# Down stage: parts of three pairs of steps held behind the last unit, the residual queued behind the loads, three pieces of sums moved there

## The chip, the core and the metric

One core of a Trainium2 chip runs the program. The core has a matrix engine (PE, with PEld for its weight loads), three engines for elementwise work (DVE, ACT, POOL), a queue engine for transfers (SP) and 16 transfer engines. Each engine takes its own instructions in the order in which they were built; an instruction that waits holds up all that stand behind it on the same engine. The metric is the device time of one execution in microseconds (us), the median over runs.

## The reference, cut to what matters

One decoder layer over 1024 tokens of width 1024, in float32: three kinds of attention, an output projection, a gated MLP with a short convolution, a gated embedding, a last norm. The change lies in the MLP:

```python
gate = h @ w_gate                       # 1024 x 2816
gate = causal_conv3(gate) + conv_b      # per column, over the last 3 tokens
r = r + (gelu(gate) * (h @ w_up)) @ w_down
```

## The kernel before

Every float32 product is done as three products of a split: an operand x is cast by ACT into a high part (`S.copy`, line 770) and DVE subtracts it from x to get a low part (line 771); `mm3` (lines 115 to 117) then multiplies high by high, high by low, low by high. So every operand that PE reads costs one ACT cast and one DVE subtraction first.

**The gate and up stage.** The 2816 hidden columns are 22 units of 128 (class `Unit` from line 910, its method `rest` from line 932). A unit takes seven products of 12 matmuls (`prod`, line 917): a two-by-two scheme with seven instead of eight block products, in which sums of blocks stand in for the eighth. The products of a unit gather in three banks of PSUM: `a`, `b` and `d`. Bank `b` takes several products one after another and is read in between: after product 7, DVE adds it to `us` (`plus(u1, "b")`, line 945), and product 4 may write into bank `b` only when that is done. Product 3 closes bank `d`, DVE adds it to `gs`, then `conv` (lines 947 to 953) runs on `gs`: ACT scales, DVE adds twice (lines 949, 951), ACT takes the gelu (line 953). DVE multiplies twice (lines 989, 990), and for an odd unit four more subtractions make the sums of the pair. POOL stores the results to DRAM: `hed` for even units, `hod`, `tad`, `tbd` for odd ones.

**The sums of the down weights.** The down projection uses the same scheme, so it needs four sums of blocks of `w_dn`. `sums_down(n, after)` (lines 1006 to 1018) makes one piece of 22: POOL loads a tile `sd` (512 KB), DVE does four operations of 128x256 on it, in the order behind `after`, and POOL stores it to `s_dram`. All pieces share one buffer, so a load waits until the store before it has landed. Unit f makes piece f-1 between its products 7 and 3, from unit 1 on; the last piece, 21, is made when the first 11 steps of the down stage are done.

**The down stage.** 77 steps (line 1062 on): 7 products of 11 steps each, a step being 12 matmuls of 128x512. Two steps make a pair g. `parts(g)` (line 1081) loads the weights of pair g (`wdr`) and, for every second pair, the stored activations of four steps (`hr`), and splits both: `hwd` and `hhd` are the casts on ACT, `lwd` and `lhd` the subtractions on DVE. These carry a raised priority, so the program that sets the order within each engine puts the parts of the first pairs ahead of the end of unit 21. `residual(i)` (line 1104) loads two tiles of the residual r (`rr`) on SP. All loads of the stage go through SP, in order.

`tc.issue_after(x)` puts what is written in its block behind instruction x, if it is on the same engine as x. It adds no semaphore.

Of the kernel before, what the change touches and what calls it, by code (L numbers as in the profile page):

```python
# [73 lines left out]
def trunk(ctx: ExitStack, tc: tile.TileContext, a, out, dbg):  # L74
# [693 lines left out]

    def hl(hi, lo, src, e=V):
        S.copy(hi, src)  # L770
        e.tensor_tensor(out=lo, in0=src, in1=hi.bitcast(F32), op=ALU.subtract)  # L771

    def sum_squares(acc, src, first, cols=slice(0, T), tag="us", e=G):
        if first:
# [16 lines left out]

    he_dram = dp.tile([NJ, P, H2], F32, name="hed")
    ho_dram, ta_dram, tb_dram = [dp.tile([NJ, P, T], F32, name=n) for n in ("hod", "tad", "tbd")]
    s_dram = dp.tile([4, NJ, P, H2], F32, name="sd")
    B = {n: [None] * 4 for n in range(1, 8)}
    acc2 = f4("ws", "acc2")
    r = [f4("r", f"r{d}") for d in range(KD)]
# [112 lines left out]
    class Unit:  # L910
# [21 lines left out]
        def rest(self):  # L932
            f, bank = self.f, self.bank
            gs, cv, us = [f4(t, f"{t}{f}") for t in ("gs", "cv", "us")]
            g0, g1 = [gs[:, half(i)] for i in range(2)]
            u0, u1 = [us[:, half(i)] for i in range(2)]

            def w(j):
                return col(C_CW + 3 * f + j)

            def copy(out, to):
                S.copy(out, bank[to])

            def plus(out, to):
                return V.tensor_tensor(out=out, in0=bank[to], in1=out, op=ALU.add)  # L945

            def conv():
                S.activation(cv, gs, AF.Identity, bias=col(C_CB + f), scale=w(2))
                V.scalar_tensor_tensor(out=cv[:, 1:], in0=gs[:, :T - 1], scalar=w(1), in1=cv[:, 1:],
                                       op0=ALU.mult, op1=ALU.add)  # L950
                V.scalar_tensor_tensor(out=cv[:, 2:], in0=gs[:, :T - 2], scalar=w(0), in1=cv[:, 2:],
                                       op0=ALU.mult, op1=ALU.add)
                S.activation(cv, cv, AF.Gelu_apprx_tanh)

            if f < 3:
                copy(g0, "b")
                plus(g0, "a")
            if f == 0:
                self.prod(5)
                copy(u1, "d")  # L960
                self.prod(3)
                copy(g1, "d")
                self.prod(6)
                plus(g1, "b")
                conv()
                self.prod(7)
                plus(u1, "b")
            else:
                if f > 2:
                    s1 = fp.tile([P, H2], F32, tag="s1", bufs=1, name=f"s1{f}")  # L970
                    self.prod(1)
                    copy(s1, "b")
                    self.prod(5)
                    copy(u1, "d")
                self.prod(6)
                copy(g1, "b")
                if f > 2:
                    self.prod(2)
                    V.tensor_tensor(out=g0, in0=bank["a"], in1=s1, op=ALU.add)
                else:  # L980
                    self.prod(5)
                    copy(u1, "d")
                self.prod(7)
                sums_down(f - 1, plus(u1, "b"))
                self.prod(3)
                plus(g1, "d")
                conv()
            self.prod(4)
            V.tensor_tensor(out=u0, in0=bank["b"], in1=cv[:, half(0)], op=ALU.mult)
            V.tensor_tensor(out=u1, in0=u1, in1=cv[:, half(1)], op=ALU.mult)  # L990
            j = f // 2
            if f % 2 == 0:
                sent[f] = G.dma_start(he_dram[j], u1)
                even.append(us)
                return
            e0, e1 = [even[j][:, half(i)] for i in range(2)]
            t1, t2 = [cv[:, half(i)] for i in range(2)]
            minus(t1, e0, e1)
            minus(t2, u0, t1)
            G.dma_start(ta_dram[j], cv)  # L1000
            minus(e0, u0, e0)
            minus(e1, u1, t2)
            sent[f] = G.dma_start(ho_dram[j], us)
            G.dma_start(tb_dram[j], even[j])

    def sums_down(n, after):

        j, c = n // 2, slice(n % 2 * 256, n % 2 * 256 + 256)
        t = cp.tile([P, 4, 256], F32, tag="rs", bufs=1, name=f"sd{n}")
        with tc.issue_after(sent[n].ins):  # L1010
            G.dma_start(t, a["w_dn"][:, j, :, c].rearrange("b p c -> p b c"))
        a11, a12, a21, a22 = [t[:, i, :] for i in range(4)]
        with tc.issue_after(after.ins):
            V.tensor_tensor(out=a22, in0=a21, in1=a22, op=ALU.add)
            minus(a21, a11, a21)
            minus(a11, a22, a11)
            minus(a12, a12, a11)
        G.dma_start(s_dram[:, j, :, c].rearrange("b p c -> p b c"), t)

    even, sent = [], {}  # L1020
    lft = [t[:, half(0)] for t in r]
# [33 lines left out]
    for f in range(3, NF):  # L1055
        with tc.high_priority(offset=3000):
            raw, A = weights_up_1(f)
            weights_up_2(f, raw, A)
        Unit(f, A).rest()


    steps = [(i, j) for i in DOWN for j in range(NJ)]
# [1 line left out]

    wd = a["w_dn"]
    OPERANDS = {1: (wd[0], he_dram), 2: (wd[1], ho_dram[:, :, half(1)]), 4: (wd[3], tb_dram[:, :, half(1)]),
                6: (s_dram[0], ta_dram[:, :, half(1)]), 3: (s_dram[1], ho_dram[:, :, half(0)]),
                7: (s_dram[2], tb_dram[:, :, half(0)]), 5: (s_dram[3], ta_dram[:, :, half(0)])}

    def load_steps(t, x0, n, which):  # L1070

        x = x0
        while x < x0 + n:
            i, j = steps[x]
            m = min(x0 + n - x, NJ - j)
            nc.sync.dma_start(t[:, x - x0:x - x0 + m, :], OPERANDS[i][which][j:j + m].rearrange("j p t -> p j t"))
            x += m

    LAST = 6 * NJ // 2

    def parts(g):

        with tc.high_priority(offset=300):
# [5 lines left out]
            load_steps(rw, 2 * g, n, 0)  # L1089
            tags = ("whi", "wlo") if g < 2 or g >= LAST and (g - LAST) % 3 else ("r", "r") if g < LAST else ("big", "big")  # L1090
            got = []
            for raw, ts in ((rw, tags), (raws[g // 2][:, g % 2 * 2:g % 2 * 2 + 2, :], ("big", "big"))):
                hi, lo = [f4(t, f"{c}{'wh'[len(got)]}d{g}", (P, 2, H2), F32R) for c, t in zip("hl", ts)]
                hl(hi[:, :n], lo[:, :n], raw[:, :n])
                got.append((hi, lo))
        return got

    r = [None] * KD
# [5 lines left out]
    def residual(i):  # L1104

        t = f4("hx", f"rr{i}", (P, 2, T))
        for d in (2 * i, 2 * i + 1):
            r[d] = t[:, d % 2, :]
            nc.sync.dma_start(r[d], r_dram[d])
        r2.append(t)  # L1110

    def done(d, h):
# [38 lines left out]
    for n, (i, j) in enumerate(steps):  # L1151
        if n % 2 == 0:
            got[n // 2] = parts(n // 2)
        if n in (4, 7, 2 * NJ, 2 * NJ + 4):
            residual((4, 7, 2 * NJ, 2 * NJ + 4).index(n))
        if n > 5 * NJ and todo or todo and j % 2:
            done(*todo.pop(0))
        (wh, wl), (xh, xl) = got[n // 2]
# [7 lines left out]
        if j == NJ - 1:  # L1166
            d0, h = TO[i]
            for d in range(4):
                x = V.tensor_tensor(out=r[d0 + d][:, half(h)], in0=bank[to][d], in1=r[d0 + d][:, half(h)], op=ALU.add)
            if i == 1:  # L1170
                sums_down(NF - 1, x)
            if i in DONE:
                todo += [(DONE[i][0] + d, DONE[i][1]) for d in range(4)]
            if i in (6, 5, 7):
# [178 lines left out]
```

## Time and profile before

| what | value |
|---|---|
| median of 3 runs | 1265.83 us (1265.01 to 1266.31) |
| the profiled execution | 1263.9 us, its span 1262.1 us |
| PE busy | 1233.6 us, 98% of the span |
| DVE busy | 906.5 us, 72% |
| ACT busy | 552.1 us, 44% |
| mean granted PE clock | 0.993 |

The span is what the profiler sees from the first instruction to the last; the execution's own time is 1.8 us longer. Times of single instructions are from the span's start. A busy PE is not a PE at its peak: overlapping matmuls count once, and a matmul at half clock counts in full. So the spacing of the starts of matmuls is read beside the busy time.

### The profile page before, as it was taken

The page shows a single profiled execution, that of the slowest core. Times are in us where ns is not written, and L with a number is a line of the kernel's source. Part 1 is how long each engine was busy: PE and PEld are TensorE (multiplying, and loading weights), DVE is VectorE, ACT ScalarE, POOL GpSimd, SP SyncE. Part 2 cuts the span into 40 slices and gives each one's busy share as a digit, 9 for nine tenths or more (in the row PEclk, how much of TensorE's full clock was granted, in tenths as well). Part 3 has the DMA queues.
Part 4 walks back from the last instruction along what each step waited for, and adds up shares of the span by engine and source line. Part 5 has one row for each costly group of instructions (what it writes and reads, how often), then busy time and mean ns, then how long its engine had stood idle before and what let it go on. Part 6 is the DMA issues. An engine that isn't in the chain of part 4 may idle for free.

```text
span 1262.1 us, 16241 instructions
## 1 busy us (share of the span) xinstructions
PE 1233.6 (98%) x6198; PEld 1034.8 (82%) x6198; DVE 906.5 (72%) x1563; ACT 552.1 (44%) x856; POOL 130.3 (10%) x162
## 2 busy tenths in 40 slices
PE   9999999999999999999999999999989999999996
PEld 7888888888888888878788888888868888888896
DVE  7996967566777477978888878778677545665676
ACT  7324233257675345644433433443353433544432
POOL 2000000011210332001111111111100000000010
PEclk9999999999999999999999999999989999999998
DMA  7100110110102844334555454455689655442132
GB/s 254 51 23 29 35 34 18 34 47 22 34 18 93 322 129 174 100 109 158 188 179 166 158 176 126 155 179 167 209 292 352 213 184 200 141 131 96 42 109 84
DMA packets 61021, 165.02 MB, mean 131 GB/s; under 512 B 6096, under 2 KB 8656, under 8 KB 60944
## 3 DMA queue, kind: packets, MB, share of 16 engines
q1 hardware_dynamic: 43744, 106.44, 25.2%
q0 software_dynamic: 15616, 55.84, 13.2%
q10 hardware_dynamic: 1584, 1.71, 0.4%
q8 instruction: 48, 0.79, 0.3%
q14 instruction: 29, 0.24, 0.1%
HBM read 119.67 MB, written 44.30 MB: 130 GB/s over the span
## 4 chain that ended last, share of the span: by engine, by line
PE 69%; DVE 7%; DMA 3%; ACT 2%; issue 2%; POOL 1%; DVEq 0%; ACTq 0%; POOLq 0%
PE d L116 6%; PE d L115 6%; PE d L117 6%; PE gb L115 5%; PE gb L116 5%; PE gb L117 5%; PE pg L115 2%; PE pg L117 2%; PE pg L116 2%; PE o L115 2%; PE o L117 2%; PE o L116 2%; PE gd L117 2%; PE gd L116 2%; PE gd L115 2%
## 5 line engine op out<-in xcount | busy, mean ns | idle before, releaser
L117 PE MATMUL d<-hhd,lwd 128*128 128x512 f32 x308 | 119.9, 389 | 0.0
L116 PE MATMUL d<-lhd,hwd 128*128 128x512 f32 x308 | 119.9, 389 | 0.0
L115 PE MATMUL d<-hhd,hwd 128*128 128x512 f32 x308 | 119.9, 389 | 0.0
L771 DVE TENSOR_TENSOR lwd<-wdr,hwd 128x1024 fp32r<-128x1024 f32 (+1 forms) x39 | 47.1, 1209 | 56.3 <-ACT hwd L770 55.2
L770 ACT CAST hwd<-wdr 128x1024 fp32r<-128x1024 f32 (+1 forms) x39 | 40.6, 1041 | 94.9 <-PE d L116 78.4
L115 PE MATMUL gb<-b,hf 128*128 128x512 f32 x176 | 70.3, 400 | 6.0 <-DVE us L945 5.6
L115 PE MATMUL gd<-b,f 128*128 128x512 f32 x176 | 68.8, 391 | 1.1 <-ACT f L770 0.6
L116 PE MATMUL gb<-b,hf 128*128 128x512 f32 x176 | 69.5, 395 | 0.0
L117 PE MATMUL gb<-b,lf 128*128 128x512 f32 x176 | 69.4, 394 | 0.0
L117 PE MATMUL gd<-b,f 128*128 128x512 f32 x176 | 68.5, 390 | 0.7 <-DVE f L771 0.7
L116 PE MATMUL gd<-b,f 128*128 128x512 f32 x176 | 68.5, 389 | 0.0
L115 PEld LDWEIGHTS d<-hhd,hwd 128*128 128x128 f32 x308 | 57.9, 188 | 12.2
L117 PEld LDWEIGHTS d<-hhd,lwd 128*128 128x128 f32 x308 | 57.8, 188 | 12.1
L116 PEld LDWEIGHTS d<-lhd,hwd 128*128 128x128 f32 x308 | 57.8, 188 | 11.8
L115 PE MATMUL pg<-hp,hpg 128*128 128x256 f32 (+1 forms) x192 | 61.7, 321 | 0.0
L116 PE MATMUL pg<-lp,hpg 128*128 128x256 f32 (+1 forms) x192 | 61.3, 320 | 0.0
L117 PE MATMUL pg<-hp,lpg 128*128 128x256 f32 (+1 forms) x192 | 61.2, 319 | 0.0
L771 DVE TENSOR_TENSOR lhd<-hr,hhd 128x1024 fp32r<-128x1024 f32 (+1 forms) x39 | 46.7, 1205 | 11.7 <-ACT hhd L770 11.5
L770 ACT CAST f<-wg 128x512 fp32r<-128x512 f32 x22 | 13.8, 625 | 77.6 <-PE gd L117 77.5
L771 DVE TENSOR_TENSOR f<-s,f 128x1024 fp32r<-128x1024 f32 x22 | 26.9, 1224 | 28.5 <-ACT f L770 28.5
L770 ACT CAST hhd<-hr 128x1024 fp32r<-128x1024 f32 (+1 forms) x39 | 39.9, 1037 | 15.0 <-PE d L116 8.5
L115 PEld LDWEIGHTS gb<-b,hf 128*128 128x128 f32 x176 | 33.6, 191 | 15.6 <-DVE us L945 6.5
(459 smaller groups left out, 3498.4 us busy)
## 6 DMA issues: line engine op xcount, KB each, us to landing
wg<-w_gu SPq DMA_DIRECT2D x22, 512.0 KB, 4.4
wu<-w_gu SPq DMA_DIRECT2D x22, 512.0 KB, 3.5
sd<-w_dn POOLq DMA_DIRECT2D x22, 512.0 KB, 5.1
sd<-sd POOLq DMA_DIRECT2D x22, 512.0 KB, 3.9
wdr<-sd SPq DMA_DIRECT2D x20, 512.0 KB, 4.0
wr_wo<-w_out SPq DMA_DIRECT2D x16, 512.0 KB, 3.8
wdr<-w_dn SPq DMA_DIRECT2D x15, 512.0 KB, 4.9
hod<-us POOLq DMA_DIRECT2D x11, 512.0 KB, 2.9
```

Of the source, the lines that this page charges most:

```text
L115: TE.matmul(o, wh, xh, start=first, stop=False, skip_group_check=on)
L116: TE.matmul(o, wh, xl, start=False, stop=False, skip_group_check=on)
L117: TE.matmul(o, wl, xh, start=False, stop=last, skip_group_check=on)
L770: S.copy(hi, src)
L771: e.tensor_tensor(out=lo, in0=src, in1=hi.bitcast(F32), op=ALU.subtract)
```

## The change

`sums_down` in the units is shifted by two: unit f makes piece f-3 from unit 3 on, and units 1 and 2 make none. Pieces 19, 20 and 21 are made in `parts(5)`, `parts(9)` and `parts(13)`, behind the last subtraction of that pair. The load of piece n is queued behind the stores of unit n+2, so that in a given unit it stands where it stood. `s_dram` becomes 11 tensors, one for each pair of pieces, and each load of two steps from it becomes two loads of 256 KB. The casts and subtractions of pairs 2, 3 and 4 are put behind the gelu of unit 21 on ACT and behind its second multiplication on DVE. The loads of the residual are queued on SP behind the loads issued so far, and two of its four calls come two and three steps later.

```diff
     def hl(hi, lo, src, e=V):
         S.copy(hi, src)
-        e.tensor_tensor(out=lo, in0=src, in1=hi.bitcast(F32), op=ALU.subtract)
+        return e.tensor_tensor(out=lo, in0=src, in1=hi.bitcast(F32), op=ALU.subtract)
...
-    s_dram = dp.tile([4, NJ, P, H2], F32, name="sd")
+    s_dram = [dp.tile([4, P, H2], F32, name=f"sd{j}") for j in range(NJ)]
...
-                S.activation(cv, cv, AF.Gelu_apprx_tanh)
+                self.ends = [S.activation(cv, cv, AF.Gelu_apprx_tanh)]
...
-                sums_down(f - 1, plus(u1, "b"))
+                x = plus(u1, "b")
+                if f > 2:
+                    sums_down(f - 3, x)
...
-            V.tensor_tensor(out=u1, in0=u1, in1=cv[:, half(1)], op=ALU.mult)
+            self.ends.append(V.tensor_tensor(out=u1, in0=u1, in1=cv[:, half(1)], op=ALU.mult))
...
-        with tc.issue_after(sent[n].ins):
+        with tc.issue_after(sent[min(n + 2, NF - 1)].ins):
             G.dma_start(t, a["w_dn"][:, j, :, c].rearrange("b p c -> p b c"))
...
-            nc.sync.dma_start(t[:, x - x0:x - x0 + m, :], OPERANDS[i][which][j:j + m].rearrange("j p t -> p j t"))
+            src = OPERANDS[i][which]
+            if isinstance(src, int):
+                m, src = 1, s_dram[j][src]
+            else:
+                src = src[j:j + m].rearrange("j p t -> p j t")
+            sp.append(nc.sync.dma_start(t[:, x - x0:x - x0 + m, :], src if len(src.shape) == 3 else src[:, None, :]))
...
+            if g in (2, 3, 4):
+                held = [tc.issue_after(x.ins) for x in last.ends]
+            else:
+                held = []
+            for x in held:
+                x.__enter__()
             for raw, ts in ((rw, tags), (raws[g // 2][:, g % 2 * 2:g % 2 * 2 + 2, :], ("big", "big"))):
                 hi, lo = [f4(t, f"{c}{'wh'[len(got)]}d{g}", (P, 2, H2), F32R) for c, t in zip("hl", ts)]
-                hl(hi[:, :n], lo[:, :n], raw[:, :n])
+                done_lo = hl(hi[:, :n], lo[:, :n], raw[:, :n])
                 got.append((hi, lo))
+            for x in held[::-1]:
+                x.__exit__(None, None, None)
+            if g in (5, 9, 13):
+                sums_down(NF - 3 + (g - 5) // 4, done_lo)
...
-        for d in (2 * i, 2 * i + 1):
-            r[d] = t[:, d % 2, :]
-            nc.sync.dma_start(r[d], r_dram[d])
+        with tc.issue_after(sp[-1].ins):
+            for d in (2 * i, 2 * i + 1):
+                r[d] = t[:, d % 2, :]
+                nc.sync.dma_start(r[d], r_dram[d])
...
-        if n in (4, 7, 2 * NJ, 2 * NJ + 4):
-            residual((4, 7, 2 * NJ, 2 * NJ + 4).index(n))
+        if n in (6, 10, 2 * NJ, 2 * NJ + 4):
+            residual((6, 10, 2 * NJ, 2 * NJ + 4).index(n))
...
-            if i == 1:
-                sums_down(NF - 1, x)
```

The first place is DVE at the end of unit 21. `us21<-gb21,us21` is the addition that product 4 waits for, `gs21`, `cv21` and the two last `us21` are the rest of the unit, `lhd` and `lwd` are subtractions for the down stage with the number of their pair. Before the change DVE had this row:

```order
L771 TENSOR_TENSOR lwd1_7501<-wdr1_7498,hwd1_7500 128x1024
L771 TENSOR_TENSOR lhd2_7541<-hr2_7532,hhd2_7540 128x1024
L771 TENSOR_TENSOR lhd3_7578<-hr2_7532,hhd3_7577 128x1024
L945 TENSOR_TENSOR us21_7343<-gb21_7345,us21_7343 128x512
L1014 TENSOR_TENSOR sd20_7413<-sd20_7413 128x256
L945 TENSOR_TENSOR gs21_7341<-gd21_7359,gs21_7341 128x512
L876 TENSOR_TENSOR sd20_7413<-sd20_7413 128x256 x3
L771 TENSOR_TENSOR lwd3_7574<-wdr3_7571,hwd3_7573 128x1024
L949 SCALAR_TENSOR_TENSOR cv21_7342<-gs21_7341,small_68,cv21_7342 128x1023
L771 TENSOR_TENSOR lwd4_7614<-wdr4_7611,hwd4_7613 128x1024
L771 TENSOR_TENSOR lwd5_7649<-wdr5_7645,hwd5_7648 128x1024
```

With the change DVE has this row at the same place:

```order
L771 TENSOR_TENSOR lwd1_7497<-wdr1_7494,hwd1_7496 128x1024
L945 TENSOR_TENSOR us21_7339<-gb21_7341,us21_7339 128x512
L1016 TENSOR_TENSOR sd18_7409<-sd18_7409 128x256
L876 TENSOR_TENSOR sd18_7409<-sd18_7409 128x256 x3
L945 TENSOR_TENSOR gs21_7337<-gd21_7355,gs21_7337 128x512
L949 SCALAR_TENSOR_TENSOR cv21_7338<-gs21_7337,small_68,cv21_7338 128x1023
L951 SCALAR_TENSOR_TENSOR cv21_7338<-gs21_7337,small_68,cv21_7338 128x1022
L991 TENSOR_TENSOR us21_7339<-gb21_7341,cv21_7338 128x512
L992 TENSOR_TENSOR us21_7339<-us21_7339,cv21_7338 128x512
L771 TENSOR_TENSOR lwd2_7533<-wdr2_7530,hwd2_7532 128x1024
L771 TENSOR_TENSOR lhd2_7537<-hr2_7528,hhd2_7536 128x1024
L771 TENSOR_TENSOR lwd3_7567<-wdr3_7564,hwd3_7566 128x1024
```

The subtractions of pairs 2 and 3 stood ahead of the addition and now stand behind the unit's last multiplication; `lwd2` stood in unit 20 before.

The second place is DVE some ten pairs later, where the last two pieces of sums now stand: `rr` are the additions to the residual when the first 11 steps are done, `lwd10` belongs to pair 10. Before the change one piece, 21, stood there:

```order
L1169 TENSOR_TENSOR rr1_7593<-d13_7473,rr1_7593 128x512
L1014 TENSOR_TENSOR sd21_7672<-sd21_7672 128x256
L876 TENSOR_TENSOR sd21_7672<-sd21_7672 128x256
L771 TENSOR_TENSOR lwd9_7804<-wdr9_7801,hwd9_7803 128x1024
L771 TENSOR_TENSOR lhd13_7961<-hr12_7915,hhd13_7960 128x1024
L876 TENSOR_TENSOR sd21_7672<-sd21_7672 128x256 x2
L771 TENSOR_TENSOR lwd10_7841<-wdr10_7838,hwd10_7840 128x1024
```

With the change DVE has this row there:

```order
L876 TENSOR_TENSOR sd20_7807<-sd20_7807 128x256 x3
L1189 TENSOR_TENSOR rr0_7574<-d10_7466,rr0_7574 128x512
L771 TENSOR_TENSOR lwd8_7766<-wdr8_7763,hwd8_7765 128x1024
L1189 TENSOR_TENSOR rr0_7574<-d11_7467,rr0_7574 128x512
L1189 TENSOR_TENSOR rr1_7656<-d12_7468,rr1_7656 128x512
L1189 TENSOR_TENSOR rr1_7656<-d13_7469,rr1_7656 128x512
L771 TENSOR_TENSOR lhd12_7929<-hr12_7919,hhd12_7928 128x1024
L771 TENSOR_TENSOR lwd9_7800<-wdr9_7797,hwd9_7799 128x1024
L771 TENSOR_TENSOR lhd13_7967<-hr12_7919,hhd13_7966 128x1024
L1016 TENSOR_TENSOR sd21_7970<-sd21_7970 128x256
L876 TENSOR_TENSOR sd21_7970<-sd21_7970 128x256 x3
L771 TENSOR_TENSOR lwd10_7844<-wdr10_7841,hwd10_7843 128x1024
```

Pieces 20 and 21 now stand in the row of subtractions, ahead of `lwd8` and of `lwd10`; piece 19 stands between the subtractions of pairs 5 to 8.

The third place is PE in unit 3, where its product 7 (`gb3<-b70`) begins. Before the change PE had this row:

```order
L115 MATMUL gd3_4893<-b33_4438,f43_4872 128x512
L116 MATMUL gd3_4893<-b33_4438,f43_4872 128x512
L117 MATMUL gd3_4893<-b33_4438,f43_4872 128x512
L115 MATMUL gb4_5019<-b10_3927,whig4_4994 128x512
L116 MATMUL gb4_5019<-b10_3927,whig4_4994 128x512
L115 MATMUL gb3_4879<-b70_4458,hf343_4868 128x512
```

With the change PE has this row there:

```order
L116 MATMUL gd3_4889<-b31_4440,f43_4868 128x512
L117 MATMUL gd3_4889<-b31_4440,f43_4868 128x512
L115 MATMUL gd3_4889<-b32_4444,f43_4868 128x512
L116 MATMUL gd3_4889<-b32_4444,f43_4868 128x512
L115 MATMUL gb3_4875<-b70_4468,hf343_4864 128x512
```

With two pieces of sums gone from units 1 and 2, the order of units 2 to 5 on PE was mixed anew: product 7 of unit 3 now begins six matmuls earlier in the row (the last four of `gd3` and two of `gb4` stand behind it).

## Rows read from the trace of the kernel before

**Rows 1.** The page's part 1 (engines) and the granted clock in 40 slices.

```profile
PE 1233.6 (98%) x6198; PEld 1034.8 (82%) x6198; DVE 906.5 (72%) x1563; ACT 552.1 (44%) x856; POOL 130.3 (10%) x162
...
PEclk9999999999999999999999999999989999999998
```

**Rows 2.** Stretches: busy us and (instructions) by engine, granted clock, transfer share, GB/s.

```profile
923.50:941.30 17.80, 13.33 (x49) 10.51 (x48) 9.39 (x13) 6.75 (x7) 0.75 (x1) 0.81 0.97 343
941.30:961.30 20.00, 20.00 (x90) 16.52 (x88) 15.57 (x18) 10.13 (x11) 2.40 (x4) 1.00 0.94 330
961.30:981.30 20.00, 20.00 (x90) 16.57 (x89) 13.02 (x16) 7.90 (x8) 0.76 (x1) 1.00 0.97 356
```

**Rows 3.** PE in order of time, end of unit 21: start, duration, instruction, [idle before].

```profile
924.02 0.39 PE L115 MATMUL ga<-b,whig 128*128 128x512 f32 x1
...
931.27 0.39 PE L117 MATMUL gd<-b,f 128*128 128x512 f32 x1
936.13 0.80 PE L115 MATMUL gb<-b,hf 128*128 128x512 f32 x1 [4.47 <-DVE us L945]
...
941.31 0.39 PE L115 MATMUL d<-hhd,hwd 128*128 128x512 f32 x1
```

**Rows 4.** DVE in order of time, the same place.

```profile
933.11 2.36 DVE L771 TENSOR_TENSOR lhd<-hr,hhd 128x1024 fp32r<-128x1024 f32 x2 [4.77 <-ACT hhd L770]
935.39 0.68 DVE L945 TENSOR_TENSOR us<-gb,us 128x512 f32<-128x512 f32 x1
935.99 0.41 DVE L1014 TENSOR_TENSOR sd<-sd 128x256 f32<-128x256 f32 x1
...
936.92 1.33 DVE L876 TENSOR_TENSOR sd<-sd 128x256 f32<-128x256 f32 x3
...
950.10 0.68 DVE L990 TENSOR_TENSOR us<-us,cv 128x512 f32<-128x512 f32 x1
```

**Rows 5.** ACT in order of time, the same place.

```profile
932.04 1.99 ACT L770 CAST hhd<-hr 128x1024 fp32r<-128x1024 f32 x2 [4.95 <-DMA hr<-hed]
```

**Rows 6.** SP's issue of the load `hr2`, and its size and time to landing.

```profile
923.78 0.38 SPq L1076 DMA_DIRECT2D hr<-hed  x1
...
hr<-hed SPq DMA_DIRECT2D x1, 1024.0 KB, 8.2
```

**Rows 7.** DVE in unit 20, from the addition of bank `d` to the second multiplication.

```profile
914.13 0.68 DVE L945 TENSOR_TENSOR gs<-gd,gs 128x512 f32<-128x512 f32 x1
...
920.58 0.68 DVE L990 TENSOR_TENSOR us<-us,cv 128x512 f32<-128x512 f32 x1
```

**Rows 8.** POOL's issue of the load in unit 21; then that load's time to landing.

```profile
922.10 0.76 POOL L1011 DMA_DIRECT2D sd<-w_dn  x1
...
DMA to landing us min/median/max: 4.3/4.3/4.3
```

**Rows 9.** Time to landing of the ten transfers of `sd`, loads and stores, 860 to 985 us.

```profile
DMA to landing us min/median/max: 3.4/4.5/7.8
```

**Rows 10.** DVE at pair 6: `lwd6`, and the first addition to the residual.

```profile
958.73 1.23 DVE L771 TENSOR_TENSOR lwd<-wdr,hwd 128x1024 fp32r<-128x1024 f32 x1 [3.00 <-ACT hwd L770]
...
969.43 0.69 DVE L1169 TENSOR_TENSOR rr<-d,rr 128x512 f32<-128x512 f32 x1 [2.90 <-PE d L117]
```

**Rows 11.** PE's waits in units 1 to 5.

```profile
557.34 0.50 PE L115 MATMUL gb<-b,hf 128*128 128x512 f32 x1 [1.14 <-DVE us L945]
...
566.86 0.50 PE L115 MATMUL gb<-b,f 128*128 128x512 f32 x1 [0.38 <-ACT gs L942]
...
607.63 0.50 PE L115 MATMUL gd<-b,f 128*128 128x512 f32 x1 [0.43 <-ACT us L942]
...
620.91 0.50 PE L115 MATMUL gb<-b,hf 128*128 128x512 f32 x1 [0.29 <-ACT gs L942]
```

**Rows 12.** DVE and ACT in units 1 and 2: the pieces of sums, and a copy that waits for a store.

```profile
557.20 0.41 DVE L1014 TENSOR_TENSOR sd<-sd 128x256 f32<-128x256 f32 x1
...
576.68 0.59 ACT L942 COPY us<-gd 128x512 f32<-128x512 f32 x1 [4.72 <-DMA tbd<-us]
```

More of the change, by code (lines that the diff above doesn't have):

```diff
@@ L1017, in sums_down @@
             minus(a12, a12, a11)
-        G.dma_start(s_dram[:, j, :, c].rearrange("b p c -> p b c"), t)
+        G.dma_start(s_dram[j][:, :, c].rearrange("b p c -> p b c"), t)
     even, sent = [], {}
@@ L1058, in trunk @@
             weights_up_2(f, raw, A)
-        Unit(f, A).rest()
+        last = Unit(f, A)
+        last.rest()
     steps = [(i, j) for i in DOWN for j in range(NJ)]
@@ L1066, in trunk @@
     OPERANDS = {1: (wd[0], he_dram), 2: (wd[1], ho_dram[:, :, half(1)]), 4: (wd[3], tb_dram[:, :, half(1)]),
-                6: (s_dram[0], ta_dram[:, :, half(1)]), 3: (s_dram[1], ho_dram[:, :, half(0)]),
-                7: (s_dram[2], tb_dram[:, :, half(0)]), 5: (s_dram[3], ta_dram[:, :, half(0)])}
+                6: (0, ta_dram[:, :, half(1)]), 3: (1, ho_dram[:, :, half(0)]),
+                7: (2, tb_dram[:, :, half(0)]), 5: (3, ta_dram[:, :, half(0)])}
     def load_steps(t, x0, n, which):
@@ L1075, in load_steps @@
             m = min(x0 + n - x, NJ - j)
-            nc.sync.dma_start(t[:, x - x0:x - x0 + m, :], OPERANDS[i][which][j:j + m].rearrange("j p t -> p j t"))
+            src = OPERANDS[i][which]
[4 more added lines that the diff above has]
+            sp.append(nc.sync.dma_start(t[:, x - x0:x - x0 + m, :], src if len(src.shape) == 3 else src[:, None, :]))
             x += m
     LAST = 6 * NJ // 2
+    sp = []
     def parts(g):
@@ L1168, in trunk @@
             for d in range(4):
-                x = V.tensor_tensor(out=r[d0 + d][:, half(h)], in0=bank[to][d], in1=r[d0 + d][:, half(h)], op=ALU.add)
-            if i == 1:
-                sums_down(NF - 1, x)
+                V.tensor_tensor(out=r[d0 + d][:, half(h)], in0=bank[to][d], in1=r[d0 + d][:, half(h)], op=ALU.add)
             if i in DONE:
```

## The prediction

> **What bounds the kernel now.** I read the page's engine shares and clock first. PE is busy 98% of the span [rows 1], so the end is set by the number of matmuls, and only stretches in which PE waits or runs slowly can be won. The clock line has an 8 in one slice besides the last [rows 1], near 930 us, the passage from the last unit to the down stage. The stretches around it show what that is: from 923.50 to 941.30 PE holds 49 matmuls at a granted clock of 0.81, while the next two stretches of 20 us hold 90 each at 1.00 [rows 2].
>
> PE in order of time gives the size. Steady matmuls of 128x512 start every (931.27 - 924.02) / 32 = 0.227 us. Then 4.86 us pass from the start at 931.27 to the next at 936.13, so 4.63 us are lost, and the row says that the addition at line 945 on DVE ended the wait. The 12 matmuls of product 4 that follow take 941.31 - 936.13 = 5.18 us, 0.43 each, half pace, in place of 2.72: the clock fell to its lower level while PE stood, and that costs 2.46 us more [rows 3]. Together **7.1 us**.
>
> Why was the addition late? Its bank was complete when product 7 ended, 12 matmuls before 931.27 plus 0.39 for the last one, so at 928.9. DVE had ahead of it two subtractions for the down stage, begun at 933.11 after an idle 4.77 us, and the addition came at 935.39 [rows 4]. Those two waited for casts on ACT, and these for a load [rows 5] that was issued at 923.78 and took 8.2 us, to 932.0 [rows 6]. So one load, early for the stage that needs it, stood in front of the unit that PE was still working on.
>
> **The change part by part.**
>
> *Holding pairs 2 to 4.* The addition now stands directly behind `lwd1`, with no down-stage subtraction ahead of it. It can run at 928.9 and is done by 929.6, before product 3 ends on PE (931.27 + 0.39 = 931.66). Product 4 then starts at 931.27 + 0.227 = 931.5 and ends at 934.2; the stage's first matmul follows there in place of 941.31. That is the 7.1 us, if nothing new waits. What is late next? Pairs 0 and 1 are split already and give 48 matmuls, 10.9 us, to 945.1. Pair 2 must be ready then. Its casts and subtractions wait for the end of unit 21. In unit 20 that tail took from 914.13 to 920.58 + 0.68 = 921.26, so 7.1 us [rows 7]; in unit 21 it starts at 931.7, hence ends at 938.8. The piece of sums in between (0.41 + 1.33 = 1.74 us, [rows 4]) runs while PE does product 3, since its load, issued at 922.10, lands 4.3 us later, at 926.4 [rows 8]. `lwd2` and `lhd2` take 2 x 1.23 us, to 941.3: 3.8 us to spare. Pairs 3, 4 and 5 follow at 2.46 us each against 24 x 0.227 = 5.45 us of PE each. The load `hr2` may come as late as 938 without harm. So the hold costs nothing here.
>
> *Loads and residual on SP.* The residual's loads move behind others and the activations for pairs 4 to 9 move ahead of `wdr7`, which now waits for the held `lwd2`, to 940. Pair 7 is needed at 934.2 + 14 x 2.72 = 972.3, so this is covered by over 30 us. The residual tiles are first used when 11 steps are done, 934.2 + 11 x 2.72 = 964.1. The split of the sums' loads into 256 KB adds issues on SP, whose casts wait for PE, not for loads; I put it at zero.
>
> *Sums in the down stage.* DVE gets eight operations of 128x256 more there (3.5 us), and the waits for three loads. After 938.8 come eight subtractions (9.8 us), then piece 19 between three more (1.74 + 3.69 us): 954.0. Then four transfers follow one another through the one buffer: store 19, load 20, store 20, load 21, with piece 20 and piece 21 on DVE (1.74 us each). A transfer of `sd` took 3.4 to 7.8 us, median 4.5 [rows 9]. By the median piece 21 is done at 954.0 + 18.0 + 3.5 = 975.5 and `lwd10`, behind it, at 976.7; by the longest at 988.7 and 989.9. PE wants pair 10 at 934.2 + 20 x 2.72 = 988.6. So 12 us to spare, or 1.3 us short. I take the median, nothing lost, since it is the middle of ten transfers in the busiest stretch.
>
> *Units 1 to 5.* Units 1 and 2 lose two pieces, 3.5 us of DVE. PE's wait at 557.34 is for an addition that stands ahead of the first piece [rows 11, 12], so it stays. The three later waits are 0.38, 0.43 and 0.29 us [rows 11]; each is followed by a first matmul that is 0.11 us slow (0.50 for 0.39 us) and has about as much lost ahead of it. All three are worth 1.1 + 3 x 0.25, so **1.9 us at most**. Against that stands the new order on PE: product 7 of unit 3 begins six matmuls earlier in the row, and it needs a copy on ACT that stands behind another which waited 4.72 us for a store to land [rows 12], a wait that the change leaves alone. If that copy comes no sooner, PE waits 6 x 0.227 = **1.4 us there**. Between +1.9 and -1.4 I take zero, near the middle.
>
> *Sum.* 1263.9 - 7.1 = 1256.8 for the profiled execution. The median is 1265.83, 1.9 us above it, so I forecast **1258.7 us**.
>
> **The rivals.**
>
> *A late stall at pair 10.* The four transfers run at their longest, pair 10 is 1.3 us late and some matmuls behind it go at half pace, at most the 2.46 us seen at 941: 3.8 us back, 1262.5. For it: one row of DVE now carries the waits of three loads, and the transfers are busy 0.94 to 0.97 there [rows 2]. Against it: all four must be slow.
>
> *The same chain, much longer: slower than before.* It must lose over 7.1 us. `lwd10` would have to come after 988.6 + 7.1 = 995.7, so four transfers must take 995.7 - 1.2 - 3.5 - 954.0 = 37.0 us, 9.3 each; from there it decides. With 11 us each it gives 6.8 us more than that and the slow matmuls, 1265.8 + 6.8 + 2.5 = 1275. For it: the 1 MB load of [rows 6] took 8.2 us in this stretch. Against it: none of ten transfers of `sd` took more than 7.8.
>
> *The stage is at the limit of its transfers.* If the loads cannot come 7.1 us earlier, what is won at 934 is waited for later and the time stays near 1265.8. For it: 0.97 of the transfer engines' time at 356 GB/s [rows 2]. The Trainium skill says the same in its page DMA: Bandwidth & Descriptors, section Bandwidth: for transfers from HBM the limit is about 358 GB/s per core, and the 356 of the trace agrees; by that rule alone the stage could not be moved forward and the sum would be 1265.8, by the rows that follow it is 1258.7. Against it: the operands stand far ahead of PE. `lwd6` ends at 959.96 [rows 10], and PE reaches pair 6 at 941.31 + 12 x 2.72 = 973.9, 14 us later; the subtraction had waited for ACT, not for a load [rows 10]. Half of that lead is used up by the change, and half is left. That the change moves nothing is hardly a case, since the row of DVE shows the addition freed.
>
> **How the numbers follow.** Forecast, with units 1 to 5 anywhere between their bounds: 0.70, with its own range from 1258.7 - 1.9 - 0.8 (spread of the runs below the median) = 1256.0 to 1258.7 + 1.4 + 0.5 = 1260.6. Stall at pair 10: 0.13, 1260.6 to 1263. Limit of the transfers, or no effect: 0.08, at 1265.8. Slower by the long chain: 0.05, 1268 to 1275. Even faster than the bounds: 0.04. From 1256.0 to 1262.5 there is the forecast and most of the stall, 0.8. About 0.2%, 2.5 us, is what a measurement of this kernel can tell from no change: faster is below 1263.3, so 0.70 + 0.13 + 0.04 = 0.87; same 0.08; slower 0.05.
>
> **What would show it right or wrong.** Right: no wait of PE over 1 us between 915 and 960, a granted clock of 1.00 there, and 88 matmul starts in any 20 us; the addition of unit 21 right behind product 7; the gelu and second multiplication of unit 21 some 8 us after product 3; `lwd2` behind them, and PE at pair 2 without a wait. The sums: POOL's last store of `sd` near 976, no wait of PE at pair 8 or 10. Units 1 to 5: PE's lost time between 530 and 640 us within 2 us of before. Wrong would be a wait of PE at pair 2 (the tail of unit 21 longer than in unit 20), a wait at pairs 8 to 12 on DVE with a load of `sd` as its end, or a stall of several us in units 3 and 4 with a lower clock behind it.

## The result, and the profile after

The changed kernel takes 1255.03 us (median of 6 runs, 1254.13 to 1256.10), the kernel before 1265.42 us on the same chip; the ratio is 0.992, with a 95% interval from 0.9907 to 0.9932. That is 10.4 us faster. The forecast was 1258.7 us with a range from 1256.0 to 1262.5: the direction and the main step came as forecast, the gain is larger than the range allowed. Measured once more in a later comparison, the changed kernel took 1255.9 us beside 1263.7 for before, 7.8 us less (0.9936, 0.9924 to 0.9949). So the gain is some 8 to 10 us, and the traces below, which give 9.3, lie between. The profiled execution took 1254.31 us, its span 1252.5 us, 9.6 us below that of before.

The page of the changed kernel, engine shares and granted clock; the slice with the 8 at 930 us [rows 1] is gone:

```profile
PE 1230.5 (98%) x6198; PEld 1033.5 (83%) x6198; DVE 906.3 (72%) x1563; ACT 551.9 (44%) x856; POOL 130.3 (10%) x162
...
PEclk9999999999999999999999999999999999999998
```

The passage from unit 21 to the down stage, as stretches of the changed kernel (busy us and instructions of PE, PEld, DVE, ACT and POOL, granted clock, transfer share, GB/s). It answers to [rows 2]: 90 matmuls in 20 us and a clock of 1.00 where before held 49 in 17.8 us at 0.81.

```profile
923.50:934.00 10.50, 10.50 (x48) 8.71 (x47) 7.48 (x10) 2.37 (x3) 0.75 (x1) 1.00 0.98 365
934.00:954.00 20.00, 20.00 (x90) 16.57 (x89) 18.27 (x20) 15.17 (x16) 2.06 (x3) 1.00 1.04 387
```

DVE of the changed kernel in order of time, same place; it answers to [rows 4].

```profile
926.37 0.69 DVE L945 TENSOR_TENSOR us<-gb,us 128x512 f32<-128x512 f32 x1 [0.64 <-PE gb L117]
926.97 0.42 DVE L1016 TENSOR_TENSOR sd<-sd 128x256 f32<-128x256 f32 x1
...
929.09 0.69 DVE L945 TENSOR_TENSOR gs<-gd,gs 128x512 f32<-128x512 f32 x1 [0.32 <-PE gd L117]
...
935.55 0.68 DVE L992 TENSOR_TENSOR us<-us,cv 128x512 f32<-128x512 f32 x1
936.15 1.22 DVE L771 TENSOR_TENSOR lwd<-wdr,hwd 128x1024 fp32r<-128x1024 f32 x1
```

The first addition now waits for PE's product 7 and for nothing else, the piece of sums stands behind it, and `lwd2` comes behind the second multiplication. PE runs through: its starts stay 0.23 us apart from unit 21 into the down stage, which begins at 931.61 in place of 941.31.

```profile
928.66 0.39 PE L117 MATMUL gd<-b,f 128*128 128x512 f32 x1
928.89 0.39 PE L115 MATMUL gb<-b,hf 128*128 128x512 f32 x1
...
931.61 0.39 PE L115 MATMUL d<-hhd,hwd 128*128 128x512 f32 x1
```

Where the 9.6 us come from is read from the starts of PE's matmuls: a spacing over 0.3 us, less the steady 0.227, is lost time. (Ahead of 500 us matmuls of other shapes run, so there the number only serves to compare kernels.) In us, by stretch of the span, one trace of each kernel:

| kernel | 0-75 | 75-500 | 500-545 | 545-640 | 640-910 | 910-1000 | 1000-end | all |
|---|---|---|---|---|---|---|---|---|
| before | 6.4 | 15.9 | 2.1 | 3.7 | 0.1 | 7.2 | 5.1 | 40.6 |
| after | 6.2 | 15.9 | 2.0 | 1.6 | 0.3 | 0 | 5.2 | 31.3 |
| hold alone | 8.1 | 16.0 | 2.0 | 3.7 | 0 | 0 | 5.1 | 34.8 |
| sums moved alone | 6.7 | 15.9 | 2.0 | 1.3 | 0 | 4.4 | 5.2 | 35.5 |
| residual and split alone | 8.2 | 16.1 | 1.9 | 3.6 | 0 | 7.2 | 5.1 | 42.2 |
| after without the residual's queue | 7.3 | 15.9 | 2.1 | 1.6 | 0 | 1.8 | 5.1 | 33.7 |

The difference of before and after, 9.3 us, is nearly all of the span's. It has two places: the passage, 7.2 us, which the prediction had at 7.1, and the first units from 545 to 640 us, 2.1 us, which it had at zero.

### The profile page after: what moved, and what is told of

Its sections match the earlier page's. It is cut to its first block, busy times and chain, and to the rows that moved or that the text cites. A ratio compares the mean times of both kernels' runs of the same rounds, so it can differ in the third digit from the quotient of the medians.

```text
span 1252.5 us, 16298 instructions
## 1 busy us (share of the span) xinstructions
PE 1230.5 (98%) x6198; PEld 1033.5 (83%) x6198; DVE 906.3 (72%) x1563; ACT 551.9 (44%) x856; POOL 130.3 (10%) x162
## 4 chain that ended last, share of the span: by engine, by line
PE 51%; DVE 1%; DMA 0%; ACT 0%; issue 0%; DVEq 0%; ACTq 0%
PE d L115 6%; PE d L117 6%; PE d L116 6%; PE gb L115 5%; PE gb L116 5%; PE gb L117 5%; PE gd L115 3%; PE gd L116 3%; PE gd L117 3%; PE pg L115 2%; PE pg L117 2%; PE pg L116 2%; PE ga L115 1%; PE ga L116 1%; PE ga L117 1%; DMA sd<-w_dn 0%
## 5 line engine op out<-in xcount | busy, mean ns | idle before, releaser
L770 ACT CAST hwd<-wdr 128x1024 fp32r<-128x1024 f32 (+1 forms) x39 | 40.6, 1040 | 76.0 <-PE d L116 66.7
L770 ACT CAST f<-s 128x1024 fp32r<-128x1024 f32 x22 | 23.1, 1052 | 51.0 <-PE gb L117 47.1
```

## The experiments

**Theory.** The hold gives the 7.1 us of the passage and nothing else. The rest comes from the first units, and there mainly from *transfers*: piece 0 of the sums no longer loads 512 KB beside the weights `wg` of unit 2, for which DVE, and behind it PE, were waiting. **Rivals.** The operations of pieces 0 and 1 on DVE cost the time in the first units; or all of the gain is the hold's; or part of it comes from the residual's new place and the split loads.

### The hold alone

Against the kernel before:

```diff
...
+            held = [tc.issue_after(x.ins) for x in last.ends] if g in (2, 3, 4) else []
+            for x in held:
+                x.__enter__()
             for raw, ts in ((rw, tags), ...
...
```

> The kernel before with the hold of pairs 2 to 4 alone: no sums moved, no residual behind loads, one array for the sums. Theory A (two separate gains): the passage gives its 7.1 us and nothing else, so 1265.4 - 7.1 = 1258.3 us; PE's lost time between 500 and 640 us stays at about 6.0, with the 1.1 us wait at product 4 of unit 1; clock 1.00 between 915 and 960. Rival B (the whole gain is the hold's, the early units moved by chance): 1255 us. Rival C (the hold needs the residual behind the loads, because SP's row else stands at a load whose buffer the held subtractions free late): a new wait of PE at one of the pairs 2 to 9, 1260 us or more.

Measured: 1257.5 us against 1264.6 for before beside it, ratio 0.9948 (0.9935 to 0.9961), so 7.1 us less. The passage loses nothing, and PE's waits from 545 to 640 us are those of before (total us, times, longest):

```profile
PE gb L115 <- DVE us L945: 1.1, 1, 1.1
PE gb L115 <- ACT gs L942: 0.7, 2, 0.4
PE gd L115 <- ACT us L942: 0.4, 1, 0.4
```

So the hold gives the passage and only that, and it needs neither of the other parts.

### The sums moved alone

Against the changed kernel:

```diff
-            if g in (2, 3, 4):
+            if g in ():
...
-        if n in (6, 10, 2 * NJ, 2 * NJ + 4):
+        if n in (4, 7, 2 * NJ, 2 * NJ + 4):
```

> The kernel after without the hold and with the residual at its old places: the sums shifted by two units, three pieces in the down stage, one array for each j. Theory A: the lost time in units 1 to 5 falls by 2.1 us to about 3.9, the passage keeps its 4.6 us wait and 2.5 us of half pace: 1265.4 - 2.1 = 1263.3 us. Rival B (all of the gain is the hold's): 1265.4. Rival C (the pieces in the down stage give something too): 1262 or less, with less lost after 940.

Measured: 1259.8 us, 0.9967 (0.9955 to 0.9980), 4.8 us under before (2.5 to 5.7 by the interval), more than the 2.1 us of theory A. Rival C has the number, 1262 or less, but not the place: the pieces in the down stage gain nothing. The first units gain what was expected, 2.4 us by the table. The other part, 2.8 us by the table, stands in the passage, where the wait became shorter. PE of this kernel, end of unit 21:

```profile
928.46 0.39 PE L117 MATMUL gd<-b,f 128*128 128x512 f32 x1
931.64 0.80 PE L115 MATMUL gb<-b,hf 128*128 128x512 f32 x1 [2.79 <-DVE us L945]
...
934.68 0.39 PE L116 MATMUL gb<-b,hf 128*128 128x512 f32 x1
```

The wait is 2.79 us where it was 4.47 [rows 3], and the slow pace behind it is over after 6 to 7 matmuls, not 12. The load `hr2` landed in 6.8 us here and in 8.2 before [rows 6]. Why it was faster is open: SP's and POOL's issues just ahead of it stand as in before, 3.1 us earlier. The landing of this load scatters: two executions of one kernel, the one with four pieces below, have 8.5 and 7.4 us. So it is not shown that the moved sums cause this second part. Whatever its cause, the changed kernel has it only once, since the hold removes this wait whole: 7.1 + 4.8 us apart, 10.4 together.

### The residual's queue and the split loads alone

Against the changed kernel (the last piece is again made behind the first 11 steps):

```diff
-            if g in (2, 3, 4):
+            if g in ():
...
-                if f > 2:
-                    sums_down(f - 3, x)
+                sums_down(f - 1, x)
...
```

> The kernel after without the hold and with the sums at their old places: only the residual behind the loads and the array of sums split in eleven with its loads. Theory A, as the prediction had it: nothing, 1265.4 within 0.5 us. Rival C (part of the 10.4 us is from here): 1264 or less.

Measured: 1263.9 us, 0.9996 (0.9987 to 1.0005): nothing, as expected. The passage waits as before:

```profile
937.43 0.79 PE L115 MATMUL gb<-b,hf 128*128 128x512 f32 x1 [4.49 <-DVE us L945]
```

### What the first units were waiting for: three runs

The place is product 4 of unit 1, PE's wait at 557.34 [rows 11]. In time order, POOL, SP and DVE of the kernel before, some 12 us earlier:

```profile
544.78 0.75 POOL L1011 DMA_DIRECT2D sd<-w_dn  x1
...
545.93 0.33 SPq L885 DMA_DIRECT2D wg<-w_gu  x1
...
550.78 0.69 DVE L876 TENSOR_TENSOR wu<-wg,wu 128x512 f32<-128x512 f32 x1 [4.15 <-DMA wg<-w_gu]
```

and of the changed kernel:

```profile
545.55 0.33 SPq L885 DMA_DIRECT2D wg<-w_gu  x1
...
549.25 0.69 DVE L876 TENSOR_TENSOR wu<-wg,wu 128x512 f32<-128x512 f32 x1 [2.99 <-DMA wg<-w_gu]
```

Before, POOL issues the load of piece 0 just ahead of SP's load of `wg`, `wg` lands in 4.8 us, and DVE stands idle for it. After it, the `wg` load has no other load beside it and lands in 3.6. The addition that PE waits for is the seventh instruction of DVE behind the one that waits, with no idle time in between. Three kernels tell the transfer from the operations. First, the changed kernel with only the load of piece 0 put back:

```diff
+                if f == 1:
+                    early[0] = load_down(0, 0)
                 if f > 2:
                     sums_down(f - 3, x)
...
```

> The kernel after with one transfer put back: the load of piece 0 (512 KB) is issued behind the first store of unit 0, as before; its four operations on DVE and its store stay in unit 3. Theory A (the transfer of piece 0 had slowed the load of wg beside it, and through it the addition that PE waits for at product 4 of unit 1): the load of wg lands in 4.5 us or more again instead of 3.6, the wait of about 1.1 us comes back, 1255.0 + 1.2 = 1256.2 us. Rival B (the operations of pieces 0 and 1 on DVE were what cost): no wait, 1255.0 us.

DVE and PE of that kernel:

```profile
551.43 0.69 DVE L876 TENSOR_TENSOR wu<-wg,wu 128x512 f32<-128x512 f32 x1 [3.71 <-DMA wg<-w_gu]
```

```profile
557.99 0.50 PE L115 MATMUL gb<-b,hf 128*128 128x512 f32 x1 [0.71 <-DVE us L945]
```

Second, before without that load:

```diff
-            G.dma_start(t, a["w_dn"][:, j, :, c].rearrange("b p c -> p b c"))
+            if n:
+                G.dma_start(t, a["w_dn"][:, j, :, c].rearrange("b p c -> p b c"))
...
+            if n == 0:
+                y, z = src[:, :256], src[:, 256:]
...
```

> The kernel before with the load of piece 0 of the sums left out: its four operations on DVE stand where they stood, with the same shapes, but read the tile u1 of unit 1, and its store stays (so piece 0 of the sums is not computed from the weights). Theory A (the transfer slowed the load of wg): wg lands in about 3.6 us, DVE's idle time ahead of line 876 falls from 4.15 to about 3.0, and PE's wait at product 4 of unit 1 falls from 1.3 us lost to 0.2. Rival B (the operations on DVE cost): the loss of 1.3 us stays. Time about 1 us below before by A, equal by B.

```profile
550.90 0.69 DVE L876 TENSOR_TENSOR wu<-wg,wu 128x512 f32<-128x512 f32 x1 [2.94 <-DMA wg<-w_gu]
```

PE, with no wait:

```profile
557.46 0.50 PE L115 MATMUL gb<-b,hf 128*128 128x512 f32 x1
```

Third, before without the four operations:

```diff
-        with tc.issue_after(after.ins):
+        if n:
+            with tc.issue_after(after.ins):
```

> The kernel before with the four operations of piece 0 on DVE left out (the piece is stored as loaded, so its sums are not made); its load and its store stay. Theory A: the 1.3 us lost at product 4 of unit 1 stay. Rival B: they go. The other losses of units 1 to 3 (0.65 at product 6 of unit 2, 0.34, 0.71 and 0.56 later) may shrink by either; time within 1 us of before.

```profile
550.57 0.69 DVE L876 TENSOR_TENSOR wu<-wg,wu 128x512 f32<-128x512 f32 x1 [4.07 <-DMA wg<-w_gu]
```

```profile
557.12 0.50 PE L115 MATMUL gb<-b,hf 128*128 128x512 f32 x1 [1.09 <-DVE us L945]
```

Together, with the loss at product 4 of unit 1 from the starts on PE:

| kernel | piece 0's load in unit 1 | its operations there | landing of `wg`, us | lost at product 4, us |
|---|---|---|---|---|
| before | yes | yes | 4.8 | 1.4 |
| before without the operations | yes | no | 4.7 | 1.4 |
| after with the load put back | yes | no | 4.3 | 1.0 |
| before without the load | no | yes | 3.5 | 0.2 |
| after | no | no | 3.6 | 0.25 |

The loss goes with the load and not with the operations, so the theory holds for this place, and it is 1.2 of the 2.1 us. Putting the load back gave 0.7 us of them, less than the 1.2 expected, with a landing of 4.3 us where 4.5 was the least expected. The other kernels of this document agree: in all 14 traces `wg` lands in 4.3 to 4.8 us with the load beside it and in 3.4 to 3.6 without, and the place loses 1.0 to 1.4 us or 0.1 to 0.3. The times alone don't tell it: 1255.6 us with the load put back (0.9932, 0.9920 to 0.9944), 1262.3 without the load (0.9986, 0.9973 to 0.9998), 1264.1 without the operations (0.9995, 0.9985 to 1.0004). Nor is it all. At product 6 of unit 2 the loss falls from 0.65 to 0.3 us in the changed kernel; it also falls to 0.3 without the operations, and to nothing without the load, so there the two can't be told apart. Without the load a new wait of 1.2 us for ACT came at 601.75. The remaining 0.9 us of the first units, spread over waits of 0.2 to 0.6 us, were not taken apart further, and their cause is open.

### After without the residual's queue

Against the changed kernel:

```diff
-        with tc.issue_after(sp[-1].ins):
-            for d in (2 * i, 2 * i + 1):
+        for d in (2 * i, 2 * i + 1):
...
-        if n in (6, 10, 2 * NJ, 2 * NJ + 4):
+        if n in (4, 7, 2 * NJ, 2 * NJ + 4):
```

> The kernel after with the residual's loads back at their old places (asked for at steps 4 and 7, not queued behind the other loads). Theory A, as in the prediction: the passage runs without a wait in either order, 1255.0 us within 0.5. Rival C (with the hold, SP's row needs the residual behind the loads, or a pair of the down stage comes late): a wait of PE between 940 and 990, 1257 us or more.

Measured: 1256.8 us, 0.9939 (0.9927 to 0.9951). Against the changed kernel this difference is too small to be told by the time, but the trace shows a new wait, where rival C had it. PE, then DVE, of this kernel:

```profile
987.27 0.39 PE L116 MATMUL d<-lhd,hwd 128*128 128x512 f32 x1
989.17 0.50 PE L117 MATMUL d<-hhd,lwd 128*128 128x512 f32 x1 [1.51 <-DVE lwd L771]
989.51 0.40 PE L115 MATMUL d<-hhd,hwd 128*128 128x512 f32 x1
```

```profile
986.17 0.42 DVE L1016 TENSOR_TENSOR sd<-sd 128x256 f32<-128x256 f32 x1 [8.53 <-DMA sd<-w_dn]
...
987.90 1.22 DVE L771 TENSOR_TENSOR lwd<-wdr,hwd 128x1024 fp32r<-128x1024 f32 x1
```

This is what the prediction's first rival described: piece 21 waits for its load, `lwd10` stands behind it and ends at 989.12, and PE goes on at 989.17. The changed kernel's chain of sums, on DVE and on POOL:

```profile
946.10 0.43 DVE L1016 TENSOR_TENSOR sd<-sd 128x256 f32<-128x256 f32 x1 [0.79 <-DMA sd<-w_dn]
...
962.79 0.42 DVE L1016 TENSOR_TENSOR sd<-sd 128x256 f32<-128x256 f32 x1 [4.26 <-DMA sd<-w_dn]
...
978.90 0.42 DVE L1016 TENSOR_TENSOR sd<-sd 128x256 f32<-128x256 f32 x1 [6.04 <-DMA sd<-w_dn]
...
980.62 3.49 DVE L771 TENSOR_TENSOR lwd<-wdr,hwd 128x1024 fp32r<-128x1024 f32 x3
```

```profile
951.23 0.75 POOL L1020 DMA_DIRECT2D sd<-sd  x1 [12.47 <-DVE sd L876]
956.87 0.75 POOL L1013 DMA_DIRECT2D sd<-w_dn  x1 [4.89 <-DVE lwd L771]
...
965.37 0.77 POOL L1020 DMA_DIRECT2D sd<-sd  x1 [0.70 <-DVE sd L876]
974.39 0.77 POOL L1013 DMA_DIRECT2D sd<-w_dn  x1 [8.25 <-DMA sd<-sd]
```

There `lwd10` ends at 980.62 + 1.22 = 981.8, and PE wants it at 931.61 + 20 x 2.72 = 986.0: 4.2 us to spare. Without the residual's queue piece 21 begins 7.3 us later, 6.2 counted from the start of the down stage (932.64 here). In the transfers between 940 and 985 us the two kernels differ so, first the changed kernel, then this one:

```profile
940.00:985.00 45.00, 45.00 (x200) 37.28 (x199) 32.06 (x40) 17.58 (x18) 4.90 (x7) 1.00 0.82 301
```

```profile
940.00:985.00 45.00, 45.00 (x200) 37.25 (x199) 27.91 (x34) 20.81 (x21) 4.42 (x7) 1.00 0.98 361
```

With the residual at its old place later loads come forward as well: five loads of the residual are issued in this stretch in place of three, and 361 GB/s flow in place of 301 while the pieces wait for theirs. So this part of the change, worth nothing by itself, is the cover of the moved sums.

### The same with piece 21 behind pair 10

Besides the edit above:

```diff
-            if g in (5, 9, 13):
-                sums_down(NF - 3 + (g - 5) // 4, done_lo)
+            if g in (5, 9, 14):
+                sums_down(NF - 3 + (g - 5) // 4, done_lo)
```

> The kernel after with the residual's loads at their old places, and piece 21 made in part 14 instead of part 13, so that its wait for its load stands behind the subtraction of pair 10 on DVE, ahead of that of pair 11. Theory A (the 1.8 us lost at 987 without the residual behind the loads are the sums' chain in front of pair 10): no loss of PE between 940 and 1000, about 1.8 us under that run. Rival C (pair 10 is late for its own weights): the loss of 1.8 us at pair 10 stays.

Measured: 1255.3 us, 0.9935 (0.9919 to 0.9952), and no loss of PE between 910 and 1000 us. DVE of this kernel: the subtraction of pair 10 has been done when the piece, still late, begins.

```profile
976.22 1.22 DVE L771 TENSOR_TENSOR lwd<-wdr,hwd 128x1024 fp32r<-128x1024 f32 x1
...
985.21 0.43 DVE L1016 TENSOR_TENSOR sd<-sd 128x256 f32<-128x256 f32 x1 [6.64 <-DMA sd<-w_dn]
```

The stall came from the piece's place in DVE's row, not from pair 10's own weights.

### The loads of three pieces made twice

Against the changed kernel:

```diff
-            G.dma_start(t, a["w_dn"][:, j, :, c].rearrange("b p c -> p b c"))
+            for k in range(2 if n >= NF - 3 else 1):
+                G.dma_start(t, a["w_dn"][:, j, :, c].rearrange("b p c -> p b c"))
```

> The kernel after with the loads of pieces 19, 20 and 21 made twice, one behind the other, so that each piece comes one landing (4.5 to 8.4 us) later. Theory A (pair 10 had 4.4 us to spare: its subtraction ended at 981.8, PE wanted it at 986.2): 3 x 4.5 = 13.5 us later at the least, so PE waits some 9 us at pair 10 and goes at half pace behind it, up to 2.5 us: 1255.0 + 9 to 11.5 = 1264 to 1267 us. By the prediction's count of 12 us to spare: 1.5 to 4 us, 1257 to 1259.

Measured: 1259.3 us, 0.9964 (0.9950 to 0.9977): 3.4 us over the changed kernel beside it, not 9 to 11. It doesn't test the reserve, because the order on DVE changed with it. DVE, then PE:

```profile
984.52 1.22 DVE L771 TENSOR_TENSOR lwd<-wdr,hwd 128x1024 fp32r<-128x1024 f32 x1
993.17 0.42 DVE L1017 TENSOR_TENSOR sd<-sd 128x256 f32<-128x256 f32 x1 [7.43 <-DMA sd<-w_dn]
...
993.97 1.22 DVE L771 TENSOR_TENSOR lwd<-wdr,hwd 128x1024 fp32r<-128x1024 f32 x1
```

```profile
983.52 0.51 PE L117 MATMUL d<-hhd,lwd 128*128 128x512 f32 x1 [0.72 <-DVE lwd L771]
995.24 0.50 PE L117 MATMUL d<-hhd,lwd 128*128 128x512 f32 x1 [0.54 <-DVE lwd L771]
```

Piece 21 is 14.3 us later, about the 13.5 expected, but the subtraction of pair 10's weights now stands ahead of it. So pair 9, behind piece 20, and pair 11, behind piece 21, waited, 2.1 and 0.8 us. The miss is one of the order, not of the chain. The reserve of 4.2 us rests on the rows above and on the run without the residual's queue.

### Four pieces in the down stage, and the changed kernel again

Against the changed kernel:

```diff
-                if f > 2:
-                    sums_down(f - 3, x)
+                if f > 3:
+                    sums_down(f - 4, x)
...
-            if g in (5, 9, 13):
-                sums_down(NF - 3 + (g - 5) // 4, done_lo)
+            if g in (5, 8, 11, 14):
+                sums_down(NF - 4 + (g - 5) // 3, done_lo)
```

> The kernel after with the sums shifted by one unit more: unit f makes piece f-4, four pieces (18 to 21) are made in parts 5, 8, 11 and 14. Theory A (early units lose by transfers and DVE work that stand there): unit 3 loses its piece, so of the 1.6 us still lost from 545 to 640 some 0.5 go; pair 10 stands behind three pieces as before and pair 14 has time for the fourth: 1254.5 us. Rival (one buffer for four pieces, each about 16 us in the stretch of full transfers: pieces 20 and 21 come late): a wait of PE on DVE at pair 10 to 16, 1258 us or more.

> The changed kernel once more, unaltered, beside the runs below: every theory expects 1255.0 us within 1 us, no loss of PE between 910 and 1000, 3.9 us lost between 500 and 640.

> The kernel with four pieces in the down stage once more, beside the changed kernel on the same chip. Its trace lost 0.7 us less between 545 and 640 than the changed kernel, so theory A: 0.5 us below it, if the wait at 604 (0.8 us) stays away in this execution too; rival (the wait at 604 comes and goes by itself, as it was away in the run with one load put back): no difference that can be told.

Measured: 1255.6 us (0.9938, 0.9925 to 0.9951), and measured once more 1256.1 (0.9939, 0.9926 to 0.9952) beside 1255.9 for the changed kernel (0.9936, 0.9924 to 0.9949). No difference in time can be told. In both traces the first units lose 0.9 and 1.0 us in place of 1.6 and 1.5, the wait for ACT near 605 being away, and no time is lost between 910 and 1000 us. That is the 0.5 us of theory A, in the traces alone, and the rival's late pieces did not come. So the kernel has no faster form in this direction that these runs could show.

## Why the prediction was off

**The passage: right.** 7.2 us by the spacing of PE's starts, 7.1 in the forecast, 7.1 by the hold alone. The steps behind it hold too: the tail of unit 21 takes from 929.09 to 936.23, 7.1 us as read from unit 20 [rows 7]; `lhd2`, behind `lwd2`, ends some 4.0 us before PE is at pair 2, where 3.8 were counted; clock 1.00 throughout.

**Units 1 to 5: the step that failed.** The term was taken at zero between +1.9 and -1.4, with the sentence that "PE's wait at 557.34 is for an addition that stands ahead of the first piece [rows 11, 12], so it stays". The addition does stand ahead of the piece's operations. But the piece's *load* is issued 12 us ahead of them on another engine, and it ran beside the very load that DVE was waiting for. The prediction counted the removed pieces by their operations on DVE alone, though two loads and two stores went with them. What it measured: 2.1 us gained in the first units, 1.2 of them at the wait that was said to stay and by that load. The prediction's own sign, PE's lost time between 530 and 640 us within 2 us of before, was just missed with 2.2. The Trainium skill has the rule that was left out, in its page Trainium Kernel Development and Optimization, section Key Constraints: transfers issued by SP, ACT and POOL run on the same 16 transfer engines and interleave. The traces agree, with 4.3 to 4.8 us for `wg` beside the other load and 3.4 to 3.6 without it. The loss of 1.4 us feared at product 7 of unit 3 did not come. The store of `tbd`, for which ACT's copy waited 4.72 us [rows 12], landed in 2.9 us in place of 5.7, and that wait fell to 2.64. It goes with the load of piece 1, which POOL issued some 2.5 to 4 us ahead of this store: in all 14 traces the store lands in 3.8 to 5.7 us where that load is there, and in 2.9 where it is not. So the wait that "the change leaves alone" did change.

**The base: a smaller error.** The sum 1263.9 - 7.1 was made for the profiled execution and then raised by 1.9 us to the median of three runs. Those three were a little high: with the three made beside the changed kernel the median is 1265.4, and in the 50 runs of later comparisons on other chips it was 1263.7 to 1264.6. For the profiled executions the right size of both terms gives 1263.9 - 7.2 - 2.1 = 1254.6, beside 1254.31 measured. For the medians it gives 1265.4 - 7.2 - 2.1 = 1256.1, beside 1255.0; no place in the traces shows the 1.1 us that are left, and as the later comparison gave 7.8 us in place of 10.4, they may be scatter.

**The sums in the down stage: hidden, but with a reserve of 4.2 us, not 12.** Pieces 20 and 21 came at 962.79 and 978.90, 16 us apart. The median landing of 4.5 us [rows 9] was taken for four transfers, as the middle of ten "in the busiest stretch". That was misread: seven of the ten were issued ahead of 923 us, and the three in the passage and the stage took 5.2, 5.1 and 7.4 us. In the changed kernel the four took 5.4, 5.8, 8.7 and 4.4 us, 24.3 in place of 18.0. The choice of zero came out, by a third of the margin that the prediction named, and without the residual's queue it would not have: luck had a part in it. (In the rival of the longer chain four transfers of 11 us are 7.0 us over 37.0, not 6.8; nothing hangs on it.)

**Loads and residual on SP: zero alone, not zero together.** The prediction put it at nothing because the residual is first used at 964 us and pair 7 had over 30 us to spare. No wait came from either, but the queue also holds transfers back while the sums need them; without it PE lost 1.8 us at pair 10. That is the first rival, whose place was right. Its price was not: behind a wait of 1.5 us only one matmul was slow, 0.11 us, and not the 2.46 us at half pace that it named as the most.

**The stage at the limit of its transfers: fallen.** The stage moved forward by 9.7 us, and its transfers came along, 387 GB/s from 934 to 954 us. So 356 GB/s was no limit, and before's own trace had shown that: 407 GB/s from 930 to 935 us and 390 from 945 to 950. The prediction took the figure of about 358 GB/s from the Trainium skill, page DMA: Bandwidth & Descriptors, section Bandwidth. The same section says of it that each of two cores gets this when both cores of a pair stream; here one core runs.

## What to carry to other kernels

A piece of work that is moved is its operations *and* its transfers: look where each of its loads and stores is issued, which may be long before its first operation and on another engine, and what lands beside it. A wait for a load that comes near a load of another queue can be a place to win, even if the work behind that other load has slack. And where a moved chain of transfers shares one buffer, put its links in the engine's row behind the work that PE needs next, and take landing times from the fullest stretch, not the median.

## What the runs showed of the hardware

- One 512 KB load (`wg`) beside another of the same size, issued some 1.2 us earlier by POOL, landed in 4.3 to 4.8 us (5 traces); without the other load in 3.4 to 3.6 (9 traces).
- What a wait of PE costs behind it did not follow from its length alone. Waits of 0.5 to 1.5 us in the units and the down stage were followed by one matmul 0.11 us slow. Longer ones were followed by a granted clock of 0.50, the lower level, for some matmuls: a wait of 2.79 us cost 1.5 us more (sums moved alone), one of 4.04 us 1.7 (without the load), and one of 4.5 us 2.5 to 2.6 in before and in the kernel with the residual and split alone, but 1.7 in the kernel without the operations. So of the 7.2 us that the passage lost in before, the 2.5 of slow pace can be less in another execution. The wait in the kernel without the operations:

```profile
935.24 0.79 PE L115 MATMUL gb<-b,hf 128*128 128x512 f32 x1 [4.50 <-DVE us L945]
```

- The first 75 us run the same code in all kernels, and PE waits 1.9 us near 66 us in all 14 traces. In eight the granted clock there stayed at 1.00 behind it; in six it was at the lower level for a while, 0.98 in the mean of the stretch, and 1.0 to 1.6 us more were lost (1.6 of the 8.1 us of the hold alone in the table). The stretch of 75 us, of the changed kernel and of the hold alone:

```profile
0.00:75.00 75.00, 70.85 (x349) 58.21 (x350) 64.03 (x112) 38.00 (x47) 7.14 (x14) 1.00 0.36 129
```

```profile
0.00:75.00 75.00, 70.42 (x339) 57.63 (x340) 63.77 (x112) 37.70 (x46) 7.14 (x14) 0.98 0.37 129
```

This is a part of the scatter between runs of one kernel, so a difference of 1 to 2 us is read from its place in the trace rather than from the times.
